# A decoder block's output and mixing products from two float16 parts, with weight squares taken at two fixed steps of each pair

## The chip, the cores and the metric

The kernel runs on one core of a Trainium2 chip. The metric is the device time of one execution in microseconds (us). TensorE (PE) multiplies; a weight load on it is listed as PEld. VectorE (DVE), ScalarE (ACT) and GpSimd (POOL) do the rest, and SyncE (SP) issues most DMAs. Each engine works through its own list of instructions in order and waits on semaphores that other engines raise.

## The reference

One decoder block on x of 1024 tokens by 1024 channels, all in float32:

```
h = rms_norm(x, g_pre_mix);  z = h @ w_in          # q, k, v, GLU input, two gates
y_attn = dilated_attention(q, k, v, bias) @ w_attn_out     # 512 -> 1024
y_conv = silu(layer_norm(conv31(u * sigmoid(gate)))) @ w_conv_out + b_conv_out
merged = sigmoid(z_ga) * y_attn + sigmoid(z_gc) * y_conv
x = x + rms_norm(merged @ w_mix_out, g_post_mix)
x = x + rms_norm(swiglu_ffn(rms_norm(x, g_pre_ffn)), g_post_ffn)
```

## The kernel before

**Products in parts.** A float32 product is made of three passes over a high and a low part of each operand: high by high, high by low, low by high. Most products use two float16 parts, which need a scale (a power of two) that keeps them in range; two products do not: that of the attention output (`ao`, eight tiles of 128 output channels, helper `unit`, L527 to L531, four row blocks each) and that of mixing (`mx`, eight row blocks, L1839). These two use two fp32r parts (in the trace `f32`), made by a plain copy to fp32r and a subtraction. A matmul has 512 moving columns in both.

**Stages.** In order: norm and first gates; 23 *pairs* (four GLU pairs, four and three gate pairs, twelve query-key pairs), of which each is one call of `winograd`; the value products with attention interleaved; the convolution's output product (`co`); the attention's output product (`ao`); mixing; 20 pairs of the FFN; the last FFN product. A pair is seven products of twelve matmuls, 28 steps (`tick`) of three matmuls. `later(n, f)` puts work n steps ahead; a generator that yields n sits n more steps out. So the order of the lists of all engines is set in the code by steps of PE's work, and a step that is moved changes what stands ahead of what on ACT, DVE and POOL.

**A pair's other work.** ACT copies three half products from PSUM (L557, L562, L567), and PE cannot go on in the same bank before each copy; ACT prescales and casts the next pair's weights (L209, L381), POOL makes their low parts (L382), ACT squares the weights after next (`peaks`, L137). DVE fills its time with the convolution's taps (L927).

**Early scales.** `early_scales` (L233) is a generator that starts with the query-key pairs. It loads the twelve value weights and the eight `co` weights one by one, squares each on ACT with a row sum (L250), one job in every 13 steps whatever the pair's own step is, and closes each group with a sum on DVE (L259), a cast on ACT (`total`, L149) and, seven steps later, a product with a matrix of ones on PE (`bound`, L156) from which DVE makes the scale.

**Merges.** Four times, `merge` (L1361) joins three groups' attention outputs on DVE (L1389, L1391, L1394) and transposes the sum on PE in eight transposes of 128 by 128 (L1405), four to a PSUM bank; ACT (L1408) and, for the last two, DVE (L1410) bring them to SBUF in strided order.

Of the kernel before, what the change touches and what calls it, by code (L numbers as in the profile page):

```python
# [18 lines left out]
T = 1024  # L19
# [52 lines left out]
class Build:  # L72
# [79 lines left out]
    def bound(self, a, p):  # L152

        nc = self.nc
        ps = self.bank(self.stag)
        nc.tensor.matmul(ps[:, 0:1], self.ones16, p, start=True, stop=True)  # L156
        nc.vector.tensor_scalar(a.bitcast(I32), ps[:, 0:1].bitcast(I32), 1, 0x7F800000,
                                op0=OP.logical_shift_right, op1=OP.bitwise_and)
        nc.vector.tensor_scalar(a, a, 2.0 ** 64, TINY, op0=OP.mult, op1=OP.max)

    def root(self, a, m):

        nc = self.nc
        ps = self.bank(self.stag)
        nc.tensor.transpose(ps[:, :128], m.to_broadcast([128, 128]), self.ident)
        nc.vector.tensor_reduce(a, ps[:, :128], AX.X, OP.max)
# [4 lines left out]
    def largest(self, k, c):  # L171

        nc = self.nc
        q, m = self.tiny(8, "pq", 2), self.tiny(1, "pm", 2)
        nc.scalar.activation(q, self.col8(c), AF.Square, scale=k)
        nc.vector.tensor_reduce(m, q, AX.X, OP.max)
        return m

    def scales(self, i):

        nc = self.nc
        t = self.tiny(5, "sc", 8)
        a, w, u = t[:, 0:1], t[:, 1:2], t[:, 2:5]
        self.bound(a, self.peak.pop(i))
        nc.vector.reciprocal(w, a)
        nc.vector.tensor_scalar(u, self.unscale[i >= self.fi0], a, None, op0=OP.mult)
        self.scale[i] = w, t[:, 2:3], t[:, 3:4], t[:, 4:5]
        if self.jobs[i][2] == "second":
            self.scale[i - 1] = self.scale[i]

# [42 lines left out]
    def early_scales(self, groups):  # L233

        nc = self.nc
        m = self.small.tile([128, 24], F32, name="em")
        t = self.small.tile([128, 5], F32, name="cs")
        self.conv_bias = self.small.tile([128, 8], F32, name="cb")
        for c, x, k in ((0, C_GLN, 32), (1, C_BLN, 1)):
            nc.scalar.activation(self.junk[:, :8], self.col8(x), AF.Square, scale=k * A_TOP, accum_out=m[:, c:c + 1])  # L240
        pa = self.total(m[:, 0:2], 2)
        yield 6
        self.bound(t[:, 0:1], pa)
        nc.vector.reciprocal(t[:, 1:2], t[:, 0:1])
        yield 2
        todo = [(e, j) for e, jobs in enumerate(groups) for j in jobs]
        x, ends = None, {len(jobs) + 2 + sum(len(y) for y in groups[:e]): e for e, jobs in enumerate(groups)}
        for n in range(2, len(todo) + 3):
            if x is not None:
                nc.scalar.activation(self.junk, x, AF.Square, scale=W_TOP, accum_out=m[:, n - 1:n])  # L250
            x = None
            if n < len(todo) + 2:
                x = self.slot()
                nc.sync.dma_start(x, self.jobs[todo[n - 2][1]][0])
            yield 3
            if n in ends:
                jobs = groups[ends[n]]
                r = self.tiny(1, "er", 2)
                nc.vector.tensor_reduce(r, m[:, n - len(jobs):n], AX.X, OP.add)  # L259
                yield 1  # L260
                p = self.total(r, 1)
                yield 6
                u = self.small.tile([128, 5], F32, name=f"es{ends[n]}")
                self.bound(u[:, 0:1], p)
                nc.vector.reciprocal(u[:, 1:2], u[:, 0:1])
                nc.vector.tensor_scalar(u[:, 2:5], self.unscale[0], u[:, 0:1], None, op0=OP.mult)
                for j in jobs:
                    self.scale[j] = tuple(u[:, i:i + 1] for i in range(1, 5))
            else:
                yield 8  # L270
        w = self.scale[groups[1][0]][0]
        nc.vector.tensor_tensor(t[:, 4:5], t[:, 0:1], u[:, 0:1], op=OP.mult)
        nc.vector.tensor_scalar(self.conv_bias, self.col8(C_BCO), t[:, 1:2], w, op0=OP.mult, op1=OP.mult)
        nc.vector.tensor_scalar(self.vun, self.scale[groups[0][0]][1], 1 / (KEEP * P_TOP), None, op0=OP.mult)
        self.act_scale, self.conv_un = t[:, 1:2], t[:, 4:5]
# [75 lines left out]
    def part(self, i, c):  # L351
# [7 lines left out]
        if i in self.f16:  # L359
# [1001 lines left out]
    def merge(self, hp, st, last):  # L1361
# [34 lines left out]
        yield 2 + 2 * late  # L1396
        if hp < 2:
            hi = self.slot()
        else:
            hi, lo = self.slot(F32R), self.slot(F32R)  # L1400
        for h in range(2):
            ps = self.bank("t")
            for i in range(4):
                u = h * 4 + i
                nc.tensor.transpose(ps[:, i * 128:(i + 1) * 128], O[0][:, u * 128:(u + 1) * 128], self.ident)  # L1405
            y = ps.rearrange("p (u m) -> p u m", u=4)
            a = hi.rearrange("p (m u) -> p u m", u=8)[:, h * 4:h * 4 + 4]
            nc.scalar.copy(a, y)  # L1408
            if hp > 1:
                nc.vector.tensor_tensor(lo.rearrange("p (m u) -> p u m", u=8)[:, h * 4:h * 4 + 4], y, f(a),  # L1410
                                        op=OP.subtract)
# [6 lines left out]

    def out_parts(self):

        for hp in range(2):
# [3 lines left out]
            self.OT[hp] = self.both(x)  # L1425
# [106 lines left out]
    def residual(self, banks, x, gain, out, gap=0):  # L1532
# [3 lines left out]
        for nh in range(2):  # L1536
            nc.scalar.activation(out[:, nh * H:(nh + 1) * H], banks[nh], AF.Square, scale=ROOT, accum_out=ss[:, nh:nh + 1])
        yield gap
        nc.vector.tensor_scalar(ss[:, 2:3], ss[:, 0:1], RMS_EPS, None, op0=OP.add)
        r = self.rstd_rows(ss[:, 1:2], ss[:, 2:3])  # L1540
        yield gap
# [46 lines left out]
def build(ctx, tc, aps):  # L1588
# [115 lines left out]
    for j in range(FIRST, 8):  # L1704
        B.glu_pair(j, glu_pairs[j - FIRST])
    for n in range(4):
        B.gate_pair(B.d_ga[2 * n:2 * n + 2], ga[n])
    for n in range(len(gc)):
        B.gate_pair(B.d_gc[2 * n:2 * n + 2], gc[n])
    B.CONV = (1, 1, 1, 0, 1)  # L1710
    es = B.bg(B.early_scales((B.early[:12], co)))
    for g in range(3):
        for hp in range(4):
            B.qk_pair(g, hp, qkj[g, hp])
# [9 lines left out]
    assert bl not in B.gens and es not in B.gens  # L1724
# [62 lines left out]
    rest = lambda: None  # L1787
    B.PIECE = 1
    B.wsplit = nc.gpsimd
    for n in range(8):  # L1790
# [14 lines left out]
    y = None  # L1805
    rest()
    B.OT = None

# [475 lines left out]
```

## Time and profile before

| | |
|---|---|
| median of 3 runs | 1608.08 us (1607.07 to 1608.25) |
| the profiled execution | 1608.3 us, of which its span is 1606.5 us and 1.8 us lie around it |
| busy | PE 1583.7, DVE 1255.2, ACT 1060.9, POOL 447.7 us |
| TensorE clock granted | 0.999 of full speed in the mean |

A busy PE means that a matmul is in flight; matmuls overlap, so their durations (379 ns for 512 float16 columns) are longer than the distance from one start to the next. What a matmul costs the program is read from that distance: from the chain of waits, which merges rows, or from the timeline.

### The profile page before, as it was taken

What the parts mean: (1) busy time and instruction counts of PE and PEld (TensorE: products, weight loads), DVE (VectorE), ACT (ScalarE), POOL (GpSimd) and SP (SyncE); (2) the same over time, 40 slices, a digit from 0 to 9 for tenths busy, and PEclk for the clock granted to TensorE, in tenths of its full rate; (3) what the DMA queues carried; (4) which work ended last, traced back from release to release, by engine and by line L of the source; (5) the groups of instructions that cost most, each with busy time, mean ns of one, the idle gap of its engine ahead of it and who ended that gap; (6) DMA issues with size and microseconds to landing.
All of it is one profiled execution on the core that took longest, in us unless ns stands there. A gap on an engine that the chain in (4) does not pass through costs nothing.

```text
span 1606.5 us, 25552 instructions
## 1 busy us (share of the span) xinstructions
PE 1583.7 (99%) x9052; PEld 897.7 (56%) x9052; DVE 1255.2 (78%) x2434; ACT 1060.9 (66%) x2024; POOL 447.7 (28%) x372
## 2 busy tenths in 40 slices
PE   8999999999999999999999999999999999999998
PEld 6744444444444799987657886444444444444443
DVE  6889999989899778888686665876666666787887
ACT  6476676678786569878753557767666666465654
POOL 0005777767777253663500300000000000000000
PEclk9999999999999999999999999999999999999999
DMA  4353333456565865677847532044443334494424
GB/s 176 109 195 119 107 137 138 142 180 221 180 192 128 248 191 155 166 224 222 250 162 275 196 115 96 27 170 151 154 168 144 124 125 149 142 386 132 155 92 164
DMA packets 162075, 265.56 MB, mean 165 GB/s; under 512 B 63665, under 2 KB 82796, under 8 KB 161948
## 3 DMA queue, kind: packets, MB, share of 16 engines
q1 hardware_dynamic: 157740, 251.77, 46.8%
q0 software_dynamic: 3920, 11.91, 2.3%
q8 instruction: 71, 1.16, 0.3%
q14 instruction: 56, 0.46, 0.1%
q10 hardware_dynamic: 288, 0.27, 0.0%
HBM read 190.05 MB, written 78.55 MB: 167 GB/s over the span
## 4 chain that ended last, share of the span: by engine, by line
PE 79%; DVE 10%; ACT 4%; POOL 2%; issue 2%; DMA 2%; SPq 0%; DVEq 0%; POOLq 0%; ACTq 0%
PE p L543 13%; PE p L545 13%; PE p L544 13%; PE p L2166 9%; PE p L1839 5%; PE p L527 3%; PE p L531 3%; PE p L529 3%; PE p L1184 3%; PE p L1188 2%; PE p L1186 2%; DVE p L927 2%; PE p L781 2%; PE p L1316 2%; PE p L1279 2%
## 5 line engine op out<-in xcount | busy, mean ns | idle before, releaser
L545 PE MATMUL p<-b,b 128*128 128x512 f16 x1032 | 391.1, 379 | 1.6 <-POOL b L382 1.6
L543 PE MATMUL p<-b,b 128*128 128x512 f16 x1032 | 390.9, 379 | 0.6 <-ACT p L1097 0.3
L544 PE MATMUL p<-b,b 128*128 128x512 f16 x1032 | 391.0, 379 | 0.0
L2166 PE MATMUL p<-b 128*128 128x512 f16 x924 | 199.9, 379 | 0.7 <-DVE b L373 0.7
L545 PEld LDWEIGHTS <-b 128*128 128x128 f16 x1032 | 100.9, 98 | 125.3 <-POOL b L382 4.0
L543 PEld LDWEIGHTS <-b 128*128 128x128 f16 x1032 | 100.9, 98 | 121.0
L544 PEld LDWEIGHTS <-b 128*128 128x128 f16 x1032 | 100.9, 98 | 117.2 <-issue 1.3
L927 DVE SCALAR_TENSOR_TENSOR p<-b,par,p 128x511 f32<-128x511 f32 (+14 forms) x232 | 164.0, 739 | 0.0
L2166 PEld LDWEIGHTS <-b 128*128 128x128 f16 x924 | 90.4, 98 | 110.0 <-issue 1.5
L527 PE MATMUL p<-b,b 128*128 128x512 f16 (+1 forms) x368 | 141.3, 384 | 1.6 <-ACT b L372 1.6
L531 PE MATMUL p<-b,b 128*128 128x512 f16 (+1 forms) x368 | 140.7, 382 | 0.4 <-DVE b L373 0.4
L529 PE MATMUL p<-b,b 128*128 128x512 f16 (+1 forms) x368 | 140.6, 382 | 0.0
L373 DVE SCALAR_TENSOR_TENSOR b<-d,sc,b 128x1024 f16<-128x1024 f32 x40 | 51.3, 1282 | 85.3 <-ACT b L372 85.3
L382 POOL TENSOR_TENSOR b<-d,b 128x1024 f16<-128x1024 f32 x44 | 94.0, 2135 | 83.7 <-ACT b L381 83.7
L1188 PE MATMUL p<-b,b 128*128 128x256 f16 x384 | 104.7, 273 | 0.0
L1186 PE MATMUL p<-b,b 128*128 128x256 f16 x384 | 104.7, 273 | 0.0
L1184 PE MATMUL p<-b,b 128*128 128x256 f16 x384 | 104.7, 273 | 0.0
L1839 PE MATMUL p<-b,b 128*128 128x512 f32 x384 | 90.1, 393 | 0.0
L1293 ACT ACTIVATE c<-c,stat 128x128 f32<-128x128 f32 (+1 forms) x192 | 84.3, 443 | 6.8 <-DVE stat L1283 6.7
L927 DVE SCALAR_TENSOR_TENSOR p<-c,pairs,p 128x511 f32<-128x511 f32 (+6 forms) x112 | 82.7, 738 | 0.0
L1283 DVE CUSTOM_DVE_ANT_0 c<-p,bt,sig 128x128 f32<-128x128 f32 (+1 forms) x192 | 70.8, 407 | 14.8 <-PE p L1279 11.8
L1839 PEld LDWEIGHTS p<-b,b 128*128 128x128 f32 x384 | 71.2, 188 | 14.4
(326 smaller groups left out, 3473.1 us busy)
## 6 DMA issues: line engine op xcount, KB each, us to landing
b<-w_in SPq DMA_DIRECT2D x30, 512.0 KB, 6.0
b<-w_v SPq DMA_DIRECT2D x24, 512.0 KB, 4.7
b<-w_fi SPq DMA_DIRECT2D x24, 512.0 KB, 6.2
d<-w_in SPq DMA_DIRECT2D x23, 512.0 KB, 3.5
dqS<-c SPq DMA_DIRECT2D x44, 256.0 KB, 2.2
b<-w_fo SPq DMA_DIRECT2D x22, 512.0 KB, 4.1
b<-w_fo SPq DMA_DIRECT2D x44, 256.0 KB, 5.4
c<-dqS SPq DMA_DIRECT2D x44, 256.0 KB, 4.0
```

The lines of the kernel that those rows point to most:

```text
L527: nc.tensor.matmul(ps, hi[:, s], a, start=kt == 0, stop=False)
L529: nc.tensor.matmul(ps, hi[:, s], b, start=False, stop=False)
L531: nc.tensor.matmul(ps, lo[:, s], a, start=False, stop=kt == nk - 1)
L543: nc.tensor.matmul(ps, hi[:, s], a, start=first and kt == 0, stop=False, skip_group_check=True)
L544: nc.tensor.matmul(ps, hi[:, s], b, start=False, stop=False, skip_group_check=True)
L545: nc.tensor.matmul(ps, lo[:, s], a, start=False, stop=kt == 3, skip_group_check=True)
L927: nc.vector.scalar_tensor_tensor(A[i][:, j:], src[i][:, :H - j], w[i], A[i][:, j:], op0=OP.mult, op1=OP.add)
L1184: nc.tensor.matmul(o, a, hi[:, s], start=kt == 0, stop=False)
L1186: nc.tensor.matmul(o, a, lo[:, s], start=False, stop=False)
L1188: nc.tensor.matmul(o, b, hi[:, s], start=False, stop=kt == KT - 1)
L1839: nc.tensor.matmul(banks[tt][nh], st, wt[:, nh * H:(nh + 1) * H], start=bool(kt == 0 and a), stop=bool(kt == KT - 1 and b))
L2166: nc.tensor.matmul(acc[t], x, y, start=first and e == 0, stop=last and e == 2, skip_group_check=True)
```

## The change

1. `ao` and `mx` weights, the merged attention outputs and the mixing operands become two float16 parts in one buffer instead of two fp32r buffers. All eight `ao` weights and the first two `mx` weights are scaled in place on ACT and their low parts made on POOL; for the other six `mx` weights ACT makes the high part and DVE the low one.
2. All 36 early weights (12 value, 8 `co`, 8 `ao`, 8 `mx`) are loaded and squared from the first gate pair on, two to a pair: loads at steps 2 and 12, squares at steps 14 and 24 (`early_pair`). Four group sums go through one cast and one product with four columns. Its steps are packed: sums, cast and product stand in neighbouring steps. The scalars that follow are spread over later steps.
3. Two small bounds (`root`) ride on the scales of two pairs; one more, of the attention outputs' squares, makes the mixing operands' scale after the fourth merge (`mix_scales`).
4. A merge squares its sum on ACT, transposes two steps later, and takes sixteen transposes of 64 rows by 128 columns instead of eight of 128 by 128, so that what comes out is in the order of use.

```diff
-    def early_scales(self, groups):
...
+    def early_start(self, groups):
...
+        self.todo = deque(enumerate(j for g in groups for j in g))
+        def sums():
+            pa, pb = self.largest(32 * A_TOP, C_GLN, C_BLN), self.largest(1.0, C_BCO)
+            self.roots.extend([(self.cs[:, 0:1], pa), (self.cs[:, 2:3], pb)])
+        self.later(13, sums)
+    def early_pair(self):
+        nc = self.nc
+        def load(after):
+            if not self.todo:
+                return
+            n, j = self.todo.popleft()
+            x = self.slot()
+            src, k, _ = self.jobs[j]
+            nc.sync.dma_start(x[:, :k], src)
+            self.later(after, lambda: nc.scalar.activation(self.junk[:, :k], x[:, :k], AF.Square, scale=W_TOP,
+                                                           accum_out=self.esum[:, n:n + 1]))
+        self.later(2, lambda: load(12))
+        self.later(12, lambda: load(12))
+    def early_scales(self):
+        for n, g in enumerate(self.groups):
+            nc.vector.tensor_reduce(r[:, n:n + 1], self.esum[:, b:b + len(g)], AX.X, OP.add)
+            b += len(g)
+            if n % 2:
+                yield 0
+        nc.scalar.copy(p, r)
+        yield 0
+        self.bound(a, p)
+        yield 1
+        nc.vector.reciprocal(w, a)
...
+        yield 24
...
+    def mix_scales(self):
+        yield 4
+        nc.vector.tensor_reduce(r, self.osq[:, :4], AX.X, OP.add)
+        yield 4
+        self.root(on, r)
...
     def part(self, i, c):
-        if i in self.f16:
+        if i in self.pre:
+            if c == 0:
+                nc.scalar.activation(r[:, :n], r[:, :n], AF.Copy, scale=self.scale[i][0])
+            nc.scalar.copy(hi[:, s], r[:, s])
+            nc.gpsimd.tensor_tensor(lo[:, s], r[:, s], hi[:, s], op=OP.subtract)
+        elif i in self.f16:
             self.scaled_parts(hi[:, s], lo[:, s], r[:, s], self.scale[i][0])
...
     def merge(self, hp, st, last):
-        yield 2 + 2 * late
+        yield 2
+        nc.scalar.activation(self.junk, O[0], AF.Square, scale=self.o_scale, accum_out=self.osq[:, hp:hp + 1])
+        self.measured += 1
+        if hp == 3:
+            assert self.measured == 4
+            self.mixing = self.bg(self.mix_scales())
+        yield 1 + 2 * late
...
-            hi, lo = self.slot(F32R), self.slot(F32R)
+            hi, lo = self.two(T)
         for h in range(2):
             ps = self.bank("t")
-            for i in range(4):
-                u = h * 4 + i
-                nc.tensor.transpose(ps[:, i * 128:(i + 1) * 128], O[0][:, u * 128:(u + 1) * 128], self.ident)
+            r = slice(h * 64, h * 64 + 64)
+            for u in range(8):
+                nc.tensor.transpose(ps.rearrange("p (m u) -> p u m", u=8)[:, u], O[0][r, u * 128:(u + 1) * 128],
+                                    self.ident[r, r])
...
-    B.f16 = {*range(glu_jobs[3][0], ao[0]), *range(B.fi0, len(J))}
-    B.early = [i for p in vj.values() for i in p] + co
-    B.pre = {*range(glu_pairs[0] - 1, min(vj[0, 0]))}
+    B.f16 = {*range(glu_jobs[3][0], len(J))}
+    B.early = [i for p in vj.values() for i in p] + co + ao + mx
+    B.pre = {*range(glu_pairs[0] - 1, min(vj[0, 0])), *ao, *mx[:2]}
...
+            if (g, hp) == (2, 3):
+                assert not B.todo and not B.roots
+                B.later(2, lambda: B.bg(B.early_scales()))
...
-            nc.vector.tensor_tensor(c[:, s], ps, c[:, s], op=OP.mult)
+            nc.vector.scalar_tensor_tensor(c[:, s], ps, B.att_un, c[:, s], op0=OP.mult, op1=OP.mult)
             nc.vector.scalar_tensor_tensor(c[:, s], y[:, s], B.conv_un, c[:, s], op0=OP.mult, op1=OP.add)
-            x = B.slot(F32R)
-            nc.scalar.copy(x[:, :H], c[:, s])
-            mop[hf][n] = x
-            rest()
-            rest = lambda x=x, c=c[:, s]: nc.vector.tensor_tensor(x[:, H:], c, f(x[:, :H]), op=OP.subtract)
+            x = mop[hf][n] = B.packed()
+            todo.append((x, c[:, s]))
+            if len(todo) > 1:
+                high(*todo[-2])
+            if len(todo) > 2:
+                low(*todo.popleft())
```

Three places show how instructions moved. Line numbers of the changed kernel differ: `winograd`'s matmuls L543 to L545 are L608 to L610, `unit`'s L527 to L531 are L592 to L596, the cast L381 is L446, and `bound`'s matmul L156 is L157.

PE in the last query-key pair of the kernel before, around its sixteenth matmul (L544 and L545 are the last two passes of one row block, L543 the first of the next):

```order
L544 MATMUL p723_5047<-b90_719,b713_4984 128x512
L545 LDWEIGHTS b713_4984
L545 MATMUL p723_5047<-b90_719,b713_4984 128x512
L543 LDWEIGHTS b713_4984
L543 MATMUL p723_5047<-b91_740,b713_4984 128x512
```

The same place in the changed kernel (`ep744` is the cast of the four group sums):

```order
L609 MATMUL p736_5082<-b90_719,b726_5018 128x512
L610 LDWEIGHTS b726_5018
L610 MATMUL p736_5082<-b90_719,b726_5018 128x512
L157 LDWEIGHTS ones16_263
L157 MATMUL p745_5125<-ep744_5104,ones16_263 128x4
L608 LDWEIGHTS b726_5018
L608 MATMUL p736_5082<-b91_740,b726_5018 128x512
```

The one product of the early scales now stands after the fifteenth matmul of this pair.

DVE at the same place in the changed kernel (L1144 is the low part of the pair before, L1113 and L1114 two scalars, L992 taps of the convolution, L283 the group sums):

```order
L1144 SCALAR_TENSOR_TENSOR c734_5076<-p733_5074,c734_5076 128x512
L1113 TENSOR_SCALAR sig_872<-sc718_4928 128x1
L1114 RECIPROCAL rsig_871<-sig_872 128x1
L992 SCALAR_TENSOR_TENSOR p663_4606<-b612_4300,par_283,p663_4606 128x498
L992 SCALAR_TENSOR_TENSOR p664_4607<-b612_4300,par_283,p664_4607 128x498
L283 TENSOR_REDUCE er743_5103<-em_1842 128x1 x4
```

The four sums stand behind two taps; in the kernel before, the taps there are L927 and no sum is among them.

ACT in the second gate pair of the kernel before, from the second copy out of PSUM on (L1020 and L1030 are sigmoids, L137 and L147 the squares of the weights after next and their sum):

```order
L562 COPY c294_2178<-p291_2175 128x512
L1020 ACTIVATE c293_2177<-c293_2177,sc274_2021 128x512
L567 COPY c295_2179<-p301_2249 128x512
L381 CAST b305_2281<-d283_2094 128x1024
L137 ACTIVATE junk_262,pk307_2303<-d302_2258 128x1024
L137 ACTIVATE junk_262,pk307_2303<-b303_2260 128x1024
L147 ACTIVATE pb308_2306<-pk307_2303 128x1
L1030 ACTIVATE c295_2179<-c295_2179,sc274_2021 128x512
L381 CAST b309_2325<-d306_2291 128x1024
```

The same in the changed kernel (L270 is a square of an early weight):

```order
L627 COPY c303_2210<-p300_2207 128x512
L1085 ACTIVATE c302_2209<-c302_2209,sc282_2045 128x512
L270 ACTIVATE junk_262,em_1842<-b306_2223 128x1024
L632 COPY c304_2211<-p312_2289 128x512
L446 CAST b316_2322<-d292_2124 128x1024
L137 ACTIVATE junk_262,pk318_2344<-d313_2298 128x1024
L137 ACTIVATE junk_262,pk318_2344<-b314_2300 128x1024
L147 ACTIVATE pb319_2347<-pk318_2344 128x1
L270 ACTIVATE junk_262,em_1842<-b311_2285 128x1024
L1095 ACTIVATE c304_2211<-c304_2211,sc282_2045 128x512
L446 CAST b320_2367<-d317_2332 128x1024
```

One square now stands between the second and the third copy, one between the pair's own squares and the cast of the next sums.

## Rows read from the trace of the kernel before

**Rows 1.** The page: busy us (share of the span) and instructions by engine.

```profile
PE 1583.7 (99%) x9052; PEld 897.7 (56%) x9052; DVE 1255.2 (78%) x2434; ACT 1060.9 (66%) x2024; POOL 447.7 (28%) x372
```

**Rows 2.** Windows: stretch, its us, busy by engine, PEclk, DMA share, GB/s.

```profile
226.24:244.39 18.15, 18.15 (x86) 8.24 (x85) 17.76 (x30) 12.32 (x19) 13.62 (x10) 1.00 0.39 145
353.35:371.85 18.50, 18.32 (x86) 8.17 (x85) 17.25 (x32) 14.53 (x23) 13.94 (x9) 1.00 0.60 207
426.32:445.38 19.06, 18.50 (x88) 8.26 (x86) 17.22 (x36) 16.59 (x28) 14.72 (x9) 1.00 0.65 201
845.00:897.20 52.20, 52.20 (x233) 40.03 (x232) 37.05 (x58) 17.23 (x36) 7.83 (x9) 1.00 0.77 276
897.20:988.70 91.50, 91.50 (x421) 74.81 (x419) 55.01 (x149) 55.95 (x114) 9.29 (x7) 1.00 0.33 119
```

**Rows 3.** Chain of waits in mixing: start us, us, what.

```profile
897.39 24.48 PE p L1839 x108
...
953.76 0.44 PE p L1569 x4
```

**Rows 4.** Chain of waits in the last FFN product.

```profile
1398.87 140.52 PE p L2166 x651
```

**Rows 5.** PE's groups in mixing: xcount, busy us, mean ns, idle before.

```profile
L1839 PE MATMUL p<-b,b 128*128 128x512 f32 x384 | 90.1, 393 | 0.0
L1569 PE MATMUL p<-ident,b 128*128 128x128 f32 x32 | 4.8, 272 | 0.0
```

**Rows 6.** Chain of waits in the third merge: four transposes.

```profile
831.37 0.44 PE p L1405 x4
```

**Rows 7.** Line L1405: duration ns min/median/max of its weight loads.

```profile
L1405 PEld LDWEIGHTS p<-ident,b x32: 138/141/142, 717.7 to 844.4; 128*128 128x128 f32 x32
```

**Rows 8.** Line L624, one moving column: weight loads, durations in ns.

```profile
L624 PEld LDWEIGHTS p<-mean_col,b x32: 187/192/192, 32.9 to 572.8; 128*128 128x128 f32 x32
```

**Rows 9.** Chain of waits at the first norm.

```profile
33.32 1.68 PE p L624 x16
```

**Rows 10.** Chain of waits around L684, a product of 33 rows.

```profile
52.80 0.74 PE p L684 x2
53.53 0.43 PE p L527
```

**Rows 11.** Line L250, the early squares: durations in ns.

```profile
L250 ACT ACTIVATE junk<-b x20: 1040/1052/1065, 331.6 to 493.7; 128x1024 bf16<-128x1024 f32 x20
```

**Rows 12.** Timeline of ACT in the second gate pair.

```profile
240.82 0.71 ACT L1030 ACTIVATE c<-c,sc 128x512 f32<-128x512 f32 x1
243.18 1.05 ACT L381 CAST b<-d 128x1024 f16<-128x1024 f32 x1 [1.66 <-POOL d L402]
```

**Rows 13.** Timeline of ACT where a pair ends late.

```profile
427.25 1.05 ACT L250 ACTIVATE junk<-b 128x1024 bf16<-128x1024 f32 x1
...
428.78 0.59 ACT L1097 COPY p<-p 128x512 f32<-128x512 f32 x1
```

**Rows 14.** Timeline of DVE in the last query-key pair.

```profile
521.70 0.73 DVE L927 SCALAR_TENSOR_TENSOR p<-c,pairs,p 128x498 f32<-128x498 f32 x1
```

**Rows 15.** Timeline of PE there: its sixteenth matmul.

```profile
521.26 0.38 PE L543 MATMUL p<-b,b 128*128 128x512 f16 x1
```

**Rows 16.** Timeline of DVE: a group sum of the early scales.

```profile
433.16 0.15 DVE L259 TENSOR_REDUCE er<-em 128x1 f32<-128x12 f32 x1
```

**Rows 17.** Timeline of ACT: the cast of the last group sum.

```profile
497.93 0.18 ACT L149 CAST pb<-er 128x1 bf16<-128x1 f32 x1
```

**Rows 18.** Who PE waited for: us in total, times, longest.

```profile
PE p L1405 <- DVE c L1329: 0.9, 1, 0.9
PE p L1316 <- DVE c L1329: 0.5, 1, 0.5
```

**Rows 19.** Chain of waits in the first merge.

```profile
717.07 0.60 DVE c L1329
...
719.79 0.66 PE p L1316 x4
```

More of the change, by code (lines that the diff above doesn't have):

```diff
@@ L169, in root, with largest @@
         nc.vector.tensor_scalar(a, a, 2.0 ** 64, TINY, op0=OP.mult, op1=OP.max)
-    def largest(self, k, c):
+    def largest(self, k, *cols):
         nc = self.nc
-        q, m = self.tiny(8, "pq", 2), self.tiny(1, "pm", 2)
-        nc.scalar.activation(q, self.col8(c), AF.Square, scale=k)
-        nc.vector.tensor_reduce(m, q, AX.X, OP.max)
+        q = [self.tiny(8, "pq", 4) for _ in cols]
+        m = self.tiny(1, "pm", 4)
+        for x, c in zip(q, cols):
+            nc.scalar.activation(x, self.col8(c), AF.Square, scale=k)
+        if len(q) > 1:
+            nc.vector.tensor_tensor(q[0], q[0], q[1], op=OP.add)
+        nc.vector.tensor_reduce(m, q[0], AX.X, OP.max)
         return m
@@ L183, in scales @@
         a, w, u = t[:, 0:1], t[:, 1:2], t[:, 2:5]
[L184 removed]
+        ps = self.bound(a, self.peak.pop(i))
         nc.vector.reciprocal(w, a)
@@ L231, in input_scales @@
             self.top.append(t[:, 1:2])
-    def early_scales(self, groups):
-        nc = self.nc
[L236 to L243, printed above, removed]
-        nc.vector.reciprocal(t[:, 1:2], t[:, 0:1])
[L245 to L275, printed above, removed]
@@ new lines, in early_start @@
+    def early_start(self, groups):
+        self.groups = groups
+        self.esum = self.small.tile([128, 40], F32, name="em")
+        self.cs = self.small.tile([128, 12], F32, name="cs")
+        self.es = self.small.tile([128, 12], F32, name="es")
+        self.conv_bias = self.small.tile([128, 8], F32, name="cb")
+        self.osq = self.small.tile([128, 8], F32, name="osq")
+        self.todo = deque(enumerate(j for g in groups for j in g))
[3 more added lines that the diff above has]
+        self.later(13, sums)
@@ L1424, in out_parts @@
             yield 11
-            self.OT[hp] = self.both(x)
+            self.OT[hp] = self.both(x, self.o_scale, True)
             x = None
@@ L1536, in residual @@
         for nh in range(2):
-            nc.scalar.activation(out[:, nh * H:(nh + 1) * H], banks[nh], AF.Square, scale=ROOT, accum_out=ss[:, nh:nh + 1])
+            nc.scalar.activation(out[:, nh * H:(nh + 1) * H], banks[nh], AF.Square, scale=self.mix_root, accum_out=ss[:, nh:nh + 1])
         yield gap
@@ L1723, in build @@
         B.channel_sum()
-    assert bl not in B.gens and es not in B.gens
+    assert bl not in B.gens
     B.banks(g=2, s=2, t=2, o=2)
@@ L1785, in build, with high, low @@
     mop = [[None] * 8, [None] * 8]
-    rest = lambda: None
+    todo = deque()
+    def high(x, c):
+        nc.scalar.activation(x[:, :H], c, AF.Copy, scale=B.mix_scale)
+    def low(x, c):
+        nc.vector.scalar_tensor_tensor(x[:, H:], c, B.mix_scale, x[:, :H], op0=OP.mult, op1=OP.subtract)
     B.PIECE = 1
@@ L1797, in build @@
             ps = B.unit(w, lambda kt: tuple(x[:, s] for x in B.OT[kt]), 4)
-            nc.vector.tensor_tensor(c[:, s], ps, c[:, s], op=OP.mult)
+            nc.vector.scalar_tensor_tensor(c[:, s], ps, B.att_un, c[:, s], op0=OP.mult, op1=OP.mult)
             nc.vector.scalar_tensor_tensor(c[:, s], y[:, s], B.conv_un, c[:, s], op0=OP.mult, op1=OP.add)
-            x = B.slot(F32R)
-            nc.scalar.copy(x[:, :H], c[:, s])
-            mop[hf][n] = x
-            rest()
-            rest = lambda x=x, c=c[:, s]: nc.vector.tensor_tensor(x[:, H:], c, f(x[:, :H]), op=OP.subtract)
-    y = None
-    rest()
+            x = mop[hf][n] = B.packed()
[4 more added lines that the diff above has]
+                low(*todo.popleft())
+    high(*todo[-1])
+    while todo:
+        low(*todo.popleft())
+    x = y = None
     B.OT = None
+    assert B.mixing not in B.gens
     W = [B.weights(mx[0])]
```

74 lines of the change are left out of this document (62 added, 12 removed).

## The prediction

> **What bounds the kernel now.** I read the page first: PE is busy for 1583.7 of 1606.5 us [rows 1]. Then windows by stage, to see where another engine could take over: in the second gate pair PE has no gap in 18.15 us while ACT works 12.32, DVE 17.76 and POOL 13.62; in the `ao` stage and in mixing PE has none either, and the next engine (DVE) has 15 and 36 us to spare; all at a granted clock of 1.00 [rows 2]. So the time is the number of PE's instructions times the distance between their starts, plus the few places where PE waits. The chain of waits gives these distances, since it merges rows that follow each other without a wait. A 512-column matmul of fp32r parts (`f32`) takes 24.48 / 108 = 0.2267 us [rows 3], one of float16 parts 140.52 / 651 = 0.2159 us [rows 4]. The difference of 0.0108 us is the gain on offer; the 379 to 393 ns that the groups give for one matmul contain overlap and would give a wrong one.
>
> The same windows show two pairs that are longer than the 18.16 us of a regular one: pair 13 by 0.35 and pair 17 by 0.90 us [rows 2]. Those are what early squares in the wrong place cost.
>
> **The change part by part**, against the profiled execution of 1608.3 us, which is 0.2 above the median.
>
> *Mixing.* 384 matmuls and 32 transposes [rows 5], four transposes 0.44 us [rows 3]: 384 × 0.2159 + 8 × 0.44 + 0.1 for the joints = 86.5 us, against 91.5 now [rows 2]. **−5.0.** It must be no less: nothing but PE's issue fills this stage. What the change puts on other engines there (the low parts of six weights and one small product per row block) goes to DVE, which has 55.01 of 91.50 us filled.
>
> *The `ao` stage.* Eight tiles × two halves × four row blocks × three passes = 192 matmuls × 0.0108 = **−2.1.** DVE there is at 37.05 of 52.20 us; a multiplication by a per-row scalar is put into an operation that exists, so its instructions don't get more. If its cover went, 15 us would have to be added first.
>
> *The transposes of the merges.* 32 of 128 by 128 at 0.44 / 4 = 0.109 us [rows 6] become 64 with 64 moving columns and a load of 64 rows by 128 columns. Nothing in the trace has this form. The moving part, with half the columns, can go down to 0.055, so below nothing this term cannot come. The load may be the slower half. L1405's load lasts 141 ns [rows 7], 51 ns less than the 192 of L624 [rows 8], whose one-column matmuls are paced by that load alone and come every 1.68 / 16 = 0.105 us [rows 9]. So the load of a transpose paces at about 0.054 us (0.105 − 0.051, an estimate), and now it hides behind 128 moving columns. I take 64 × 0.055 = 3.5 us, as much as now: **0**; the upper end is a full 0.109 each, +3.5. I take the lower end because the whole load of L1405 is the nearer row, being a transpose's.
>
> *Their tile height.* A product of another height than 128 rows stands in the trace only at L684 (33 rows, 384 columns): two take 0.74 us, where 2 × 3 × 0.109 would be 0.65, and the matmul of 128 rows after them takes 0.43 instead of 0.23 [rows 10]. That is 0.09 + 0.20 = 0.29 us per visit. The merges make eight visits: **+2.0** (0.25 each, since a batch of eight has more to overlap with), ends 0 and 2.3. The Trainium skill speaks against the change here too ("TensorEngine Tiling (Array Packing)", section "Key Properties"): a change of the tiling mode drains the engine. The rows of L684 agree with their 0.29 us; without that rule's effect, the term would be nothing.
>
> *Three more products* (two small bounds and that of mixing) of 128 by 128 at 0.109: **+0.3.** Two ride on a bank that is in use, so no wait comes with them.
>
> *The squares.* 36 instead of 20, at 1.05 us each [rows 11], two to each of 18 pairs. In a gate pair ACT has 18.15 − 12.32 = 5.8 us idle; the first square lands where ACT stands still now, since before the cast L381 it waits 1.66 us for POOL [rows 12], and the second behind L147. So they cost PE nothing there. In the query-key pairs steps 14 and 24 fall in the same gaps. What they replace did cost: in pair 17 a square at 427.25 held up the copy L1097, for which PE waited [rows 13]. Both long pairs should end at the regular length: **−1.25** (ends 0, if other work is late next, and −1.25). Their 16 more loads of 0.5 MB stand on SP's queue behind free slots, at a DMA share of 0.39 to 0.65 [rows 2].
>
> *The new product of four totals.* PE reaches the sixteenth matmul of the last query-key pair at 521.26 us [rows 15]. In the changed order the product stands just ahead of it, and it needs the cast of four sums that DVE starts only after two taps. In the kernel before DVE is through with the taps ahead of this place at 521.70, when it starts the next one [rows 14]. Four sums at 0.10 to 0.15 [rows 16], a cast at 0.18 [rows 17]: ready at 522.4, so PE stands for 1.2 us. Behind it stands the whole pair. **+1.2**, ends 0 (DVE runs ahead of PE here, since the stalls of pair 17 are gone) and 1.5.
>
> *The first merge.* PE waits 0.9 + 0.5 us there for DVE's L1329 [rows 18], between 717.07 and 719.79 [rows 19]. The transposes now stand two steps later, when the sum has long been there: **−0.6** (ends −1.4, both waits gone, and +1, a new one for the bank).
>
> Sum: −5.0 − 2.1 + 0 + 2.0 + 0.3 − 1.25 + 1.2 − 0.6 = −5.4, so 1602.9 us in this execution and **1602.7 us** against the median of 1608.1, 0.3% less. The times below go by the median too.
>
> **Rivals.**
>
> *The load paces the half-height transposes.* Then they cost 0.105 to 0.109 each, 3.3 to 3.5 us more: 1602.7 + 3.4 = 1606.1, no change that can be told. For it: L624's one-column matmuls, which are bound by a load of the same 128 columns, come at 0.105 [rows 9], nearly what a whole transpose takes. Against: a transpose's load is 51 ns shorter. The Trainium skill would have it so ("TensorE: Matmul & The Clock Gate", section "LDWEIGHTS (loading the stationary operand)"): the time of a load goes by its columns and not by its rows, and a load of 32 by 128 takes as long as one of 128 by 128. By that rule the 64 transposes would cost those 3.4 us more. The trace has no load of fewer rows at 128 columns to hold against it.
>
> *Switches and the new wait are free.* Height changes hide behind the matmuls that drain anyway and the sums come ahead of PE: 1602.7 − 2.0 − 1.2 = 1599.5. For it: DVE's idle time in that pair; against: L684's rows, and the two taps ahead of the sums [rows 10, 14].
>
> *The steps of the squares are bad ones.* Slower: in a pair where a prescale, a copy out of PSUM and a square meet on ACT, PE waits for the copy. Price: the mean loss of pairs 13 and 17, 0.63 us, in all 18 pairs is 11.3, counted from the regular length: 1602.7 + 11.3 = 1614.0. It decides from a loss of 0.48 us per pair on (8.6 us in all, which brings the time past 1611.3). For it: those two pairs, and ACT's 16.59 of 19.06 us in pair 17, where the convolution's work has come in. Against: most pairs of the kernel before that hold a square have the regular length, and the 1.66 us of standstill.
>
> **How the numbers follow.** Forecast 0.50 (own range 1600.7 to 1604.9), load-paced transposes 0.25, free switches 0.12, bad steps 0.09; 0.04 for what I don't see. A measurement of this kernel can tell 0.2%, 3.2 us, from no change: below 1604.9 is faster, above 1611.3 slower. Of the forecast 0.46 lies below 1604.9, with the free switches' 0.12 that is 0.58 and some of the load-paced case when the new wait is small (0.03): 0.61. Slower is the bad steps, 0.09, of which little ends within, and 0.01 of the rest: 0.09. The remaining 0.30 is no change. The range goes from 1599.5 to 1607.0 (load-paced, with 0.3 more at the new wait and both waits of the first merge kept, 0.6); it leaves out the bad steps and the outermost of the rest.
>
> **What would show it.** Mixing at 86.5 us and 192 `ao` matmuls at 41.5 show the first two terms; if a stage were longer with PE waiting for DVE or ACT, the conversion costs have come onto the path. The distance between two half-height transposes tells 0.055 from 0.109; the first matmul after a batch, 0.2 us later than usual or not, tells the drain. The waits of PE in the last query-key pair show the new product's. Pairs 4 to 22 at 18.16 us show the squares hidden; a loss of half a us in each would make the forecast wrong on the slow side. The waits for L1329 show the first merge.

## The result and the profile after

The changed kernel takes 1612.01 us (median of 10 runs, 1611.21 to 1612.70), the kernel before in the same series 1607.74: a ratio of 1.0026 (95% interval 1.0017 to 1.0036). It is slower by 0.26%, where 0.3% faster was forecast. The profiled execution took 1611.28 us, the second fastest of the ten; its span is 1609.1.

The page, against [rows 1] and [rows 5]: busy time, and the group of mixing's matmuls.

```profile
PE 1579.1 (98%) x9085; PEld 847.1 (53%) x9085; DVE 1260.7 (78%) x2458; ACT 1086.0 (67%) x2071; POOL 451.6 (28%) x377
...
L1933 PE MATMUL p<-b,b 128*128 128x512 f16 x384 | 84.5, 379 | 0.0
```

PE has 4.6 us less work than before and a span that is 2.6 us longer: 7.2 us more of standing. Where it stands is in the view of PE's waits (us in total, times, longest), against [rows 18]; the first line is the kernel's start, as in the kernel before.

```profile
PE p L846 <- ACT b L820: 6.0, 1, 6.0
PE p L1646 <- ACT b L1638: 3.6, 2, 2.9
...
PE p L167 <- DVE sc L158: 1.5, 2, 1.1
PE p L1646 <- ACT b L1652: 1.5, 1, 1.5
...
PE p L608 <- DVE c L1092: 1.0, 1, 1.0
PE p L157 <- ACT ep L287: 0.9, 1, 0.9
PE p L1381 <- DVE c L1394: 0.8, 1, 0.8
PE p L1476 <- DVE c L1394: 0.8, 1, 0.8
```

L1646 are the transposes of the normalised row blocks in mixing and at the FFN's start, L167 the small bounds, L1092 a sum that a pair's PSUM bank waits for. Windows, against [rows 2]: the first three gate pairs, which hold early squares (pairs 4, 5 and 6, counted from 0), pair 17, the `ao` product after its last merge, and mixing.

```profile
188.60:208.26 19.66, 18.49 (x87) 8.14 (x86) 19.56 (x34) 14.52 (x25) 11.99 (x8) 1.00 0.51 174
208.26:227.84 19.58, 18.45 (x87) 8.34 (x86) 17.86 (x33) 15.28 (x26) 14.72 (x10) 1.00 0.58 205
227.84:246.68 18.84, 18.46 (x88) 8.38 (x87) 18.29 (x33) 14.29 (x23) 13.61 (x10) 1.00 0.53 194
428.23:446.38 18.15, 18.15 (x86) 8.25 (x85) 16.66 (x31) 14.52 (x25) 14.39 (x10) 1.00 0.64 186
852.25:900.17 47.92, 47.92 (x225) 21.72 (x223) 38.32 (x55) 24.89 (x44) 18.63 (x19) 1.00 0.94 366
900.17:989.86 89.69, 86.75 (x421) 41.21 (x420) 56.10 (x157) 55.84 (x110) 0.21 (x1) 1.00 0.17 60
```

Mixing shows the case in one line: 86.75 us of work, as forecast (86.5), in 89.69 us. From these rows and the starts of the pairs the bill can be drawn up (a minus is time saved against the kernel before):

| term | forecast | measured, us |
|---|---|---|
| mixing | −5.0 | −1.8 (work −4.75, a wait of 2.94) |
| start of the FFN, to the next pair | 0 | +2.0 (47.5 for 45.5) |
| `ao` product | −2.1 | −2.1 (222 matmuls in 47.92: 0.2159 each) |
| half-height transposes and tile height | 0 and +2.0 | +2.3 |
| three more products | +0.3 | +2.2 (pairs 5 and 6 by 1.43 and 0.67, 0.11 before mixing) |
| sums for two of them | none | +0.8 (pair 4: 19.66, before 18.82) |
| squares, long pairs 13 and 17 | −1.25 | −1.25 in this profile |
| product of four totals | +1.2 | +1.1 |
| first merge, and what is left of the value stage | −0.6 | +0.5 |

That is +3.8, and from the first pair's start to the first pair of the FFN the traces differ by 924.18 − 920.44 = 3.7 us. The rest (−0.6 ahead of it, −0.5 behind) lies outside what the change moves.

Part of the −1.25 is lost in most executions, in pair 16. The changed kernel's own profile shows no wait there, but nine of the eleven profiles of it and its variants show one of 0.15 to 1.08 us for L1144, and pair 16 then takes 18.46 to 19.40 us instead of 18.15. The chain of waits in one of the nine (the variant with later transposes; start us, us, what):

```profile
418.56 0.83 SPq L269
...
419.99 6.55 DMA b<-w_in
...
426.62 1.16 ACT junk L137 x2
...
428.09 0.61 ACT junk L270 x2
428.70 0.49 ACT c L1143
...
429.22 0.70 DVE c L1144
```

L269 is the load of an early weight. The load of a later pair's weights is issued behind it and lands 15.0 to 16.0 us after the pair's start in the nine, 14.6 and 14.8 in the two without a wait. ACT squares these weights (L137), then comes an early square (L270), and only then the operation that L1144 needs. So an early load and an early square stand on the path here; no run took them out of it.

### The profile page after: what moved, and what is told of

The parts are those of the page before. It is cut to its first block, busy times and chain, and to the rows that moved or that the text cites. A ratio compares the mean times of both kernels' runs of the same rounds, so it can differ in the third digit from the quotient of the medians.

```text
span 1609.1 us, 25677 instructions
## 1 busy us (share of the span) xinstructions
PE 1579.1 (98%) x9085; PEld 847.1 (53%) x9085; DVE 1260.7 (78%) x2458; ACT 1086.0 (67%) x2071; POOL 451.6 (28%) x377
## 4 chain that ended last, share of the span: by engine, by line
PE 76%; DVE 13%; ACT 6%; issue 3%; DMA 1%; POOL 1%; DVEq 0%; SPq 0%; ACTq 0%; POOLq 0%
PE p L608 14%; PE p L609 14%; PE p L610 14%; PE p L2260 9%; PE p L592 3%; PE p L596 3%; PE p L594 3%; DVE p L992 3%; PE p L846 2%; PE p L1249 2%; PE p L1251 2%; PE p L1253 2%; DVE b L438 2%; PE p L1381 2%; PE p L1344 2%
## 5 line engine op out<-in xcount | busy, mean ns | idle before, releaser
L610 PE MATMUL p<-b,b 128*128 128x512 f16 x1032 | 391.5, 379 | 1.3 <-POOL b L447 1.3
L609 PE MATMUL p<-b,b 128*128 128x512 f16 x1032 | 391.4, 379 | 0.0
L608 PE MATMUL p<-b,b 128*128 128x512 f16 x1032 | 391.3, 379 | 0.0
L610 PEld LDWEIGHTS <-b 128*128 128x128 f16 x1032 | 100.8, 98 | 124.7 <-POOL b L447 3.3
L608 PEld LDWEIGHTS <-b 128*128 128x128 f16 x1032 | 101.0, 98 | 122.0 <-issue 1.2
L992 DVE SCALAR_TENSOR_TENSOR p<-b,par,p 128x511 f32<-128x511 f32 (+14 forms) x232 | 164.2, 740 | 0.0
L592 PE MATMUL p<-b,b 128*128 128x512 f16 (+1 forms) x368 | 140.6, 382 | 1.6 <-ACT b L437 1.6
L596 PE MATMUL p<-b,b 128*128 128x512 f16 (+1 forms) x368 | 140.2, 381 | 0.4 <-DVE b L438 0.4
L1933 PE MATMUL p<-b,b 128*128 128x512 f16 x384 | 84.5, 379 | 0.0
L992 DVE SCALAR_TENSOR_TENSOR p<-c,pairs,p 128x511 f32<-128x511 f32 (+6 forms) x112 | 82.8, 739 | 0.0
L438 DVE SCALAR_TENSOR_TENSOR b<-c,fs,b 128x512 f16<-128x512 f32 x77 | 57.6, 748 | 24.5 <-ACT b L437 24.4
```

What stands on the lines that cost most here:

```text
L438: self.nc.vector.scalar_tensor_tensor(lo, x, w, hi, op0=OP.mult, op1=OP.subtract)
L592: nc.tensor.matmul(ps, hi[:, s], a, start=kt == 0, stop=False)
L596: nc.tensor.matmul(ps, lo[:, s], a, start=False, stop=kt == nk - 1)
L608: nc.tensor.matmul(ps, hi[:, s], a, start=first and kt == 0, stop=False, skip_group_check=True)
L609: nc.tensor.matmul(ps, hi[:, s], b, start=False, stop=False, skip_group_check=True)
L610: nc.tensor.matmul(ps, lo[:, s], a, start=False, stop=kt == 3, skip_group_check=True)
```

## Experiments

All start from the changed kernel; "changed" below is its 1612.0 us, and the ratios are against the kernel before. That took 1607.14 to 1607.46 us in these series and 1607.74 in the changed kernel's, so up to 0.6 us of each difference is not the edit's, and most of the intervals overlap the changed kernel's. What an edit did to a wait is therefore read from its trace. Line numbers shift by one to three between the variants.

**The transposes in mixing later.**

```diff
-            yield 8
+            yield 14 if tt == 3 else 8
```

> The transposes of the first four row blocks in mixing stand six steps (about 3.9 us of matmuls) later than in the changed kernel; nothing else differs. Chain theory: float16 made PE's part of four row blocks 2.0 us shorter and the squares and scalars made the norms' serial chain on ACT and DVE longer, so that PE came to the transposes before the fourth normalised block; with the later place the wait of 3.1 us goes and mixing takes 86.5 to 87 us instead of 89.7. As the chain itself is no shorter, part may come back where the second four blocks are transposed (waits of 0.8 and 1.5 us now): in all 1 to 3 us less than the changed kernel. Rival (the low parts and scalings put on DVE and ACT fill the stage): PE waits elsewhere in mixing, the stage stays at about 89.7 and the total moves by less than 0.5 us.

1613.63 us (1.0038, 1.0026 to 1.0051): 1.6 more. Neither theory had this. The wait for L1638 in mixing went, and one of the same size (2.9 us) came four transposes later. ACT's timeline there (an entry's last bracket is its idle time and what ended it):

```profile
961.33 0.67 ACT L1652 ACTIVATE b<-p,hg 128x512 f32<-128x512 f32 x1
964.63 1.06 ACT L1636 ACTIVATE b<-d 128x1024 f32<-128x1024 f32 x1 [2.63 <-DVE d L1625]
...
966.97 1.15 ACT L1638 ACTIVATE b<-d,rr 128x1024 f32<-128x1024 f32 x1 [0.87 <-DVE rr L1605]
968.03 0.70 ACT L437 ACTIVATE b<-b,sc 128x512 f16<-128x512 f32 x1
968.64 0.60 ACT L1520 CAST b<-b 128x512 f16<-128x512 f32 x1
969.15 0.68 ACT L1652 ACTIVATE b<-p,hg 128x512 f32<-128x512 f32 x1
```

The second copy out of the transposes' bank (L1652) is written behind the next block's norm (L1636, L1638) and ACT keeps the order, so PE waits for its bank. So the backlog of the norms on ACT reaches PE at this place too. That leaves the time where it was; for the 1.6 us more, this profile shows pair 16 at 19.40 us, and a granted clock of 0.58 in the 4.0 us after the wait, worth about 1.7 us (4.0 × 0.42, an estimate).

**The norm of the second row block four steps later.** The first two blocks of mixing end together.

```diff
+        if tt == 1:
+            yield 4
         x2 = self.ring()
         yield from self.residual(banks, x, self.g_mix, x2)
```

> Mixing's first two row blocks end at one point, and their norms are written alternately on ACT and DVE; here the second block's norm is written four steps behind the first's, and nothing else differs from the changed kernel. Chain theory: the first block's operations no longer stand behind the second's, the two are through 1 to 2 us sooner than the 17.3 us after the end of their matmuls, all later blocks follow in line, and PE's wait of 3.1 us falls by as much (to 1 to 2 us): 1 to 3 us less than the changed kernel. Rival (the two chains fill ACT or DVE together, so that order doesn't matter): the fourth block is ready when it was, and the wait stays at 3.1 us.

1609.38 us (1.0015, 1.0006 to 1.0024), 2.6 less, or 2.0 when each is taken against the kernel before in its own series. The window of mixing, and below it PE's waits from there into the FFN:

```profile
900.74:987.89 87.15, 86.74 (x421) 41.23 (x420) 56.04 (x157) 55.84 (x110) 0.22 (x1) 1.00 0.19 64
```

```profile
PE p L1648 <- ACT b L1654: 1.5, 1, 1.5
PE p L1648 <- ACT b L1640: 1.1, 2, 0.7
```

Mixing takes 87.15 us; of the two waits for a normalised block (L1640), 1.1 us in all, the longer one of 0.7 stands at the FFN's start, so 0.4 of 2.9 is left in mixing, and mixing is 2.5 us shorter than in the changed kernel (89.69). The busy times of DVE (56.04) and ACT (55.84) are those of the changed kernel (56.10 and 55.84): only the order differs. So it was the chain and not the amount of work.

**One operation out of the chain.**

```diff
-        nc.vector.tensor_tensor(r, r, self.mix_un, op=OP.mult)
...
+    nc.vector.tensor_scalar(B.g_mix, B.g_mix, B.mix_un, None, op0=OP.mult)
```

> The product of each row block's norm with the mixing scale (one DVE operation of 0.16 us, 0.195 from start to start, in the chain of every block) is left out, and the gain row is multiplied by that scale once instead. Chain theory: the fourth normalised block is ready 4 x 0.195 = 0.8 us sooner, so PE's wait of 3.1 us in mixing falls to 2.3 and the wait of 0.65 us for the last block at the start of the FFN goes: 0.8 to 1.5 us less than the changed kernel. Rival (DVE's or ACT's whole work in the stage sets it, not the chain): the wait changes by under 0.3 us.

1610.68 us (1.0021, 1.0011 to 1.0031), 1.3 less (1.0 against the kernel before in each series). The wait fell from 2.94 to 2.17, 0.77 where 4 × 0.195 = 0.78 was worked out, and the one for the last block (0.65) went:

```profile
PE p L1645 <- ACT b L1637: 2.2, 1, 2.2
PE p L1645 <- ACT b L1651: 1.5, 1, 1.5
```

**Mixing in fp32r again.** Only the parts' type, with the same scales.

```diff
-            self.hl[i] = self.two(T) if i in self.f16 else (self.slot(F32R), self.slot(F32R))
+            self.hl[i] = self.two(T) if i in self.f16 and i not in self.mx else (self.slot(F32R), self.slot(F32R))
...
-            x = mop[hf][n] = B.packed()
+            x = mop[hf][n] = B.slot(F32R)
```

> The mixing product's weights and operands are two fp32r parts again, made with the same scales and by the same engines as in the changed kernel (its squares, scalars and extra products all stay). Chain theory: PE's part of the stage takes 5.0 us more again, the transposes come when the fourth block is ready, so mixing takes 91.5 to 92 us without a wait over 0.5 us there (89.7 with 3.1 us of waiting in the changed kernel), and the waits at the start of the FFN shrink from 2.3 to about 0.5 to 1: the total changes by less than 1 us, although 384 matmuls are slower by 0.0108 us each. Rival (the scalings and the extra operations make the wait, not PE's speed): the wait stays and the total is 4 to 5 us more.

1613.13 us (1.0036, 1.0023 to 1.0048), 1.1 more, just over the bound given; the waits for the normalised blocks and for the bank shrink to 0.8 and 0.5. So 384 matmuls at 0.0108 us less, 4.2 us by themselves, were worth about 1 us here.

**The small bounds in a bank of their own.**

```diff
-        if self.roots:
-            self.root(*self.roots.popleft(), ps[:, 128:256])
...
+            self.later(24 + 28 - 13, lambda: self.root(self.cs[:, 0:1], pa))
+            self.later(24 + 56 - 13, lambda: self.root(self.cs[:, 2:3], pb))
```

> The two small bounds are taken at step 24 of the second and third gate pair in a bank of their own, instead of right behind the weights' bound in the same bank. Theory of the shared bank: PE's transpose waited until DVE had read the bound from that bank (1.13 and 0.38 us); in a bank of its own it waits for nothing, pair 5 takes 18.3 instead of 19.6 us and pair 6 18.3 instead of 18.8, together 1.5 to 1.9 us less. Rival (the transpose waits for its operand, which DVE makes late): the waits stay, whatever the bank, and the total with them.

1610.28 us (1.0018, 1.0009 to 1.0028), 1.7 less. The waits for L158 are gone (pairs 5 and 6: 18.27 and 18.26 us). The edit moves the bounds to a later step as well as to another bank, so it doesn't part the two; the changed kernel's timelines of PE and DVE do:

```profile
209.55 0.17 PE L157 MATMUL p<-pb,ones 128*128 128x1 bf16 x1
210.85 0.32 PE L167 MATMUL p<-ident,pm 128*128 128x128 f32 x1 [1.13 <-DVE sc L158]
```

```profile
209.35 1.38 DVE L992 SCALAR_TENSOR_TENSOR p<-b,par,p 128x498 f32<-128x498 f32 x2
210.64 0.16 DVE L158 TENSOR_SCALAR sc<-p 128x1 int32<-128x1 int32 x1
```

The bound's reader on DVE (L158) stands behind two taps, and PE's next write to that bank waits for the reader. It is not the operand `pm` that comes late: DVE had made it by 201.1 us.

**The sums later.**

```diff
-        self.later(13, sums)
+        self.later(13 + 4 * 28, sums)
```

> The squares and sums of the two small bounds' parameters (six small operations on ACT, three on DVE) stand four pairs later, in the eighth pair that holds early squares' loads or bounds instead of the first; nothing else differs. Theory: in the first gate pair DVE, which has no idle time, falls 0.9 us behind by those three sums (0.69 + 0.16 + 0.15 us), so PE waits 0.96 us for L1092; without them pair 4 takes 18.8 us as in the kernel before instead of 19.66, and the bounds' waits of 1.13 and 0.38 us move four pairs on with them: in all about 0.8 us less than the changed kernel, or nothing if the new place is as full. Rival (the two early squares hold ACT up and with it DVE): pair 4 stays at 19.66.

1612.6 us (1.0032, 1.0020 to 1.0043), no less, where 0.8 less was expected; but pair 4 took 18.82 us, so the sums and not the squares had made it long, and the two waits moved to pairs 9 and 10 (1.1 and 0.3). The total is not comparable to a us: in this profile the matmuls after the wait in mixing ran at a lower clock (last section), and PE waited 1.0 for L1144.

**The product of the totals later.**

```diff
         nc.scalar.copy(p, r)
-        yield 0
+        yield 5
         self.bound(a, p)
```

> The product of the four totals stands five steps (about 3.2 us) later behind its cast than in the changed kernel. Theory: PE waited 1.07 us in the last query-key pair for that cast; with the later place it does not wait, the pair is 1.07 us shorter and nothing is late next: 1.0 to 1.1 us less than the changed kernel. Rival (the scalars that follow, now later, hold up the value products): a new wait at the start of the value stage, total unchanged.

1611.31 us (1.0029, 1.0018 to 1.0040), 0.7 less, within the spread of the runs, so the time alone does not show the 1.07. In the profile PE waits for nothing in that pair, nothing is late in the value stage, and from the last pair to the first of the FFN it is 1.0 us shorter (517.36 for 518.35).

**Whole transposes, single elements.** As in the kernel before, but to float16.

```diff
-                nc.tensor.transpose(ps.rearrange("p (m u) -> p u m", u=8)[:, u], O[0][r, u * 128:(u + 1) * 128],
-                                    self.ident[r, r])
+                nc.tensor.transpose(ps[:, i * 128:(i + 1) * 128], O[0][:, u * 128:(u + 1) * 128], self.ident)
...
+            a = hi.rearrange("p (m u) -> p u m", u=8)[:, h * 4:h * 4 + 4]
```

> The merges take eight transposes of 128 by 128 again, and ACT and DVE bring them to SBUF in strided order, here as float16; all else as in the changed kernel. Sum of terms: a batch of eight half-height transposes with its entry costs 0.73 us against 0.44, so eight batches give back 8 x 0.29 = 2.3 us. Rival (the strided float16 writes are slow enough to hold up the ao product or the banks): part or all of it comes back as waits around the merges, 0 to 1 us less in all.

1619.33 us (1.0074, 1.0061 to 1.0086), 7.3 more than changed: the rival, and beyond it. ACT's and DVE's copies take 2.5 us each:

```profile
L1480 ACT ACTIVATE b<-p,cs x4: 2534/2538/2556, 838.1 to 856.2; 128x512 f16<-128x512 f32 x4
L1481 DVE SCALAR_TENSOR_TENSOR b<-p,cs,b x4: 2491/2502/2511, 840.7 to 858.8; 128x512 f16<-128x512 f32 x4
```

PE waits for DVE behind these copies in the `ao` stage, where the changed kernel shows no such wait:

```profile
PE p L592 <- DVE b L1854: 3.3, 1, 3.3
PE p L592 <- DVE osq L168: 2.0, 1, 2.0
```

Not all of the loss is these waits. In this profile, itself 1.7 us above the median, the granted clock was 0.75 from 850.6 to 857.5 us, and 0.72 from 860 to 866 and from 966 to 972; the changed kernel's windows of these stages show 1.00. By PE's busy time in the three stretches that is some 4.5 us (an estimate).

**Whole transposes, runs of four.**

```diff
+                nc.tensor.transpose(ps.rearrange("p (m i) -> p i m", i=4)[:, i], O[0][:, u * 128:(u + 1) * 128], self.ident)
...
+            a = hi.rearrange("p (m u) -> p m u", u=8)[:, :, h * 4:h * 4 + 4]
```

> The merges take eight transposes of 128 by 128 again, written to PSUM with a stride of four, so that ACT and DVE write runs of four elements (8 bytes of float16) instead of single ones or whole rows. What is told apart: e4 lost 7.3 us against the kernel before since single float16 elements 16 bytes apart took 2.5 us per 128x512 instead of 0.7. If the cost goes by the writes' runs, it is near 0.7 to 0.8 us here, the tile height no longer changes, and 8 x 0.29 = 2.3 us come back: 1609.7. Rival (any strided float16 write is slow, 1.3 us or more): no gain or a loss around the merges.

1610.55 us (1.0019, 1.0010 to 1.0029), 1.5 less, of the 2.3 expected; in this profile the clock fell to 0.57 after the wait in mixing (last section). The same copies, as fast as those of whole rows in the changed kernel (687 and 747 ns):

```profile
L1480 ACT ACTIVATE b<-p,cs x4: 687/687/687, 836.9 to 849.9; 128x512 f16<-128x512 f32 x4
L1481 DVE SCALAR_TENSOR_TENSOR b<-p,cs,b x4: 740/746/750, 838.5 to 850.6; 128x512 f16<-128x512 f32 x4
```

**All together**, from the second block's norm to the runs of four, with the bounds and sums both apart and four pairs later.

> All mendings at once: small bounds in a bank of their own and four pairs later, the product of the four totals five steps later, whole transposes with runs of four, the gain folded, the second row block's norm four steps later. If the terms add up: 1.6 (bounds) + 0.8 (sums) + 1.07 (product) + 2.3 less what the first merge takes (1.5 measured) + 1.3 (gain) + 1 to 2 (row blocks) = 7 to 8.5 us less than the changed kernel's 1612.0, so 1603.5 to 1605, 3 to 4 us less than the kernel before. Rival (each mended wait uncovers another behind it): 1607 to 1609.

1602.5 us (0.9974 of the kernel before, 0.9963 to 0.9985): 9.5 us less than changed (8.9 against the kernel before in each series), where 7 to 8.5 had been added up, and 4.6 less than before. The window of mixing, and what is left of PE's wait for a copy out of PSUM at the FFN's start:

```profile
895.38:982.15 86.77, 86.53 (x421) 41.34 (x420) 55.59 (x152) 56.20 (x112) 0.20 (x1) 1.00 0.19 66
```

```profile
PE p L1645 <- ACT b L1651: 1.5, 1, 1.5
```

Its 1602.5 us are the forecast's number by chance: the terms are others (the tile height no longer changes, two waits that the forecast held are gone).

## Why the prediction was wrong

**The step that failed** is the sentence on mixing that "nothing but PE's issue fills this stage". PE had no gap there in the kernel before, but it had no room either. ACT's and PE's timeline of the kernel before, at its first transposes:

```profile
952.46 1.15 ACT L1561 ACTIVATE b<-d,rr 128x1024 f32<-128x1024 f32 x1 [0.87 <-DVE rr L1529]
...
953.60 0.60 PE L1569 MATMUL p<-ident,b 128*128 128x128 f32 x4
```

The last normalised block was ready at 953.61 and the four transposes began at 953.60; the fourth, which reads this block, stands three starts of 0.109 behind, so the room was about 0.3 us. Each norm is a chain of some 9 us that changes between ACT and DVE six times, ACT takes the blocks one after the other, and the first two come at once. In the changed kernel the fourth block is ready 37.2 us after the first squares (before 36.0), and PE arrives after 33.8 (before 36.0). The 2.2 us that float16 gave PE by then and the 1.15 us by which the chain grew, less 0.3 for the three transposes that go ahead, make the wait of 2.94 to within 0.1. Same row, changed kernel:

```profile
955.59 1.15 ACT L1638 ACTIVATE b<-d,rr 128x1024 f32<-128x1024 f32 x1 [0.87 <-DVE rr L1605]
956.65 0.67 ACT L1613 ACTIVATE d<-p,cs 128x512 f32<-128x512 f32 x1
956.80 0.33 PE L1646 MATMUL p<-ident,b 128*128 128x128 f32 x1 [2.94 <-ACT b L1638]
```

The backlog runs on: the last block's norm starts 2.4 us after its matmuls and costs the FFN's start the 2.0 us of the table. The forecast had compared DVE's 55 us with 91.5, a sum over the stage, where the chain's end decides (and ACT, with 55.95 us, not DVE, was the next engine there). The second block's later norm and the folded gain, which touch the chain alone, took 2.5 and 0.8 us of the wait away.

Of the 9.2 us between the two columns of the table, mixing and the FFN's start hold 5.2, the three products 1.9, the first merge and what is left of its stage 1.1, and the sums 0.8.

**Three more products**: "two ride on a bank that is in use, so no wait comes with them" had the reason upside down. A bank in use is one that the next write waits for. In a bank of their own and at a later step the 1.5 us of waits were gone.

**The sums** for those bounds were not priced at all: three small DVE operations, 0.9 us, in pair 4, where DVE had next to nothing free. The window that the prediction read for the second gate pair, with 17.76 of 18.15 us filled [rows 2], is pair 6, the third. Pair 4 in the kernel before:

```profile
189.26:208.08 18.82, 18.48 (x86) 8.16 (x85) 18.75 (x31) 12.63 (x19) 12.69 (x9) 1.00 0.41 140
```

DVE was busy for 18.75 of 18.82 us. With the sums later pair 4 has its old length.

**Right** were the `ao` product, the wait at the product of the totals (1.07 for 1.2) and, in the main, the early squares, which hold up only pair 16, and that not in every execution; its mean loss over the eleven profiles, 0.6 us, is half of the 1.25 gained. Eight of the 36 squares, those of `ao`, are of 128x512 and took 0.61 us, not the 1.05 of the forecast. The rival of bad steps fell: pair 4 is long by the sums (it was no regular pair before, either, with 18.82 us), and in the changed kernel's profile pairs 7 to 22 are regular but for the wait at the totals.

**The merges' transposes** cost 0.29 us a batch more than those of the kernel before, in all 2.3 for the forecast's 2.0. Two errors offset each other in it: a transpose starts every 0.062 us and not every 0.055, 0.4 us more for the 64, and the change of height is left with 1.9 us, 0.23 a batch for 0.25. PE's timeline of one batch:

```profile
847.20 0.38 PE L596 MATMUL p<-b,b 128*128 128x512 f16 x1
847.51 0.71 PE L1476 MATMUL p<-ident,b 64*128 64x64 f32 x8
848.15 0.39 PE L592 MATMUL p<-b,b 128*128 128x512 f16 x1
```

Eight take 0.64 us to the next start, against 0.44 for the four whole ones, and the way in takes 0.31 us from the matmul ahead instead of 0.216. So the load-paced rival (8 × 0.105 = 0.84) is out: eight in 0.64 are 0.08 each, the change of height included. By the Trainium skill ("TensorE: Matmul & The Clock Gate", section "LDWEIGHTS (loading the stationary operand)") these loads of 64 by 128 would take as long as whole ones. In the trace they do last as long (a median of 138 ns, and 141 for L1405's [rows 7]), but they don't pace the transposes, as the rival had it: within a batch these start every 0.062 us (a median), whole ones every 0.109.

**The first merge** kept its waits, 0.8 and 0.8 us for L1394 where [rows 18] had 0.9 and 0.5: its transposes wait for DVE's work on the attention, not for the merge's own sum, so two steps more gained nothing.

## What to carry to other kernels

Before a stage is costed by the engine that is busy all through it, look at what is ready just in time in it: at each place where that engine takes another's result, compare the end of the one with the start of the other. Up to such a place a faster matmul gains no more than the margin there, and a serial chain of small operations on two engines has a speed of its own that no busy share shows. What is added to a chain counts once for every block that goes through it in turn (4 × 0.195 us here), and a write into a bank that another engine still has to read can be a wait.

## What was not expected of the hardware

Writing float16 elements singly, 16 bytes apart, took ACT 2.54 and DVE 2.50 us per 128x512, against 0.69 and 0.75 in runs of four or whole rows. Single float32 elements, 32 bytes apart, took ACT 1.10 (L1484 of the same kernel). So the copy to the narrower type was 2.3 times slower; about 0.1 us of that is the scale that it applies (0.69 against 0.58 for L1485, without one, in the changed kernel). Why the narrow single writes are so slow was not tried.

After PE's wait of 2.9 us in mixing the clock stayed up in some profiles and fell in others. Windows before and after the wait, first the changed kernel, then that with the later sums (the granted clock is the number behind the five busy times):

```profile
946.00:953.30 7.30, 7.30 (x35) 3.37 (x34) 4.38 (x15) 2.83 (x7) 0.00 (x0) 1.00 0.31 97
957.00:961.00 4.00, 4.00 (x22) 2.09 (x21) 2.27 (x9) 3.77 (x10) 0.00 (x0) 1.00 0.08 26
```

```profile
947.00:954.80 7.80, 7.80 (x39) 3.65 (x37) 4.47 (x15) 3.20 (x8) 0.00 (x0) 1.00 0.33 103
958.00:962.00 4.00, 3.94 (x12) 1.60 (x13) 2.01 (x9) 3.21 (x9) 0.00 (x0) 0.59 0.18 67
```

At 0.59, near the lower level of 1.2 GHz, 12 instructions went through in 4 us instead of 22. The profiles of the kernels with the later transposes and with the runs of four show it too (0.58 and 0.57), that of the whole transposes three times, and that of the bounds apart after the waits of the first merge (0.66 from 724 to 729 us). What decides between the two was not tried. It adds some 1.7 us (4 us × 0.41 to 0.43, an estimate) to a wait in some executions, and is one reason why totals of variants that keep this wait don't add up to a us.
